# Two blocks on one core: the first sublayer's start in a new order, and all low parts of weights on VectorE

## The chip, the cores and the metric

The kernel runs on one core of a Trainium2 chip. The metric is the device time of one execution, in microseconds. Three runs of the kernel before took 2796.14, 2797.77 and 2798.36 us; their median is 2797.77 us. One execution was profiled as well; its span, from its first to its last instruction, is 2793.1 us.

## The reference

Two transformer blocks on 512 tokens of 1024 features, in float32. Only the beginning matters in detail:

```python
c_act = silu(c)
mod = (c_act @ w_mod[l] + b_mod[l]).reshape(1, 9, 1024)
h = rmsnorm(x, g_norm[l, 0]) * (1 + mod[:, 1]) + mod[:, 0]
x = x + 0.5 * mod[:, 2] * swiglu(h, w_ffn1_gu[l], w_ffn1_down[l])
```

Then, for each of two layers, a mixer (windowed attention, a gated recurrence and short convolutions), and a second feed-forward part; then a second block: a mixer of latent attention (a softmax over 768 keys) and gated linear attention, also over 256 context tokens, and a feed-forward part whose gate goes through a 3 x 3 convolution. Each part begins with an RMS norm, scaled and shifted by vectors that are products of a condition with a matrix.

## The kernel before

Features lie on the partitions, tokens along the free axis: x is eight chunks `X[0..7]` of 128 x 512. A weight comes as units of 128 x 1024 or less, in their order of use, by DMA from SyncE into four buffers (`raw`). Products are made in three passes of rounded parts: each weight and each input is split into a high part (`whi`, a rounded copy, made by ScalarE) and a low part (`wlo`, the value less its high part), and high x high, high x low and low x high are added up in one PSUM bank. There are four `whi` and four `wlo` buffers, so splits run up to three units ahead.

`split_next` (line 454) makes the parts of the next unit. The low part is VectorE's (`split`, line 509) in most of the first block. For the first eight units, for the second block's mixer (key `x`) and for its feed-forward part (key `20`) it is GpSimd's (line 465); the eight have 896 columns, most of the others 1024.

The unit list also holds the rows of `w_mod`: a modulation vector's 128 values are a dot product on VectorE of a 128 x 1024 tile with the condition's row (line 515), and a read of the accumulator, both in `dot`. `mod_unit` adds the bias (line 527) and, for the scale, makes (1 + m) g (line 529).

`start` (line 1986) is the head. Products of ones run first; the squares of the eight chunks are made by ScalarE and added up by VectorE in two sums (lines 572 to 577); eight one-column products add them over the features (line 1994); root and reciprocal follow, `diag` puts the 512 values on a diagonal (line 612), and `spread` brings them to all partitions by a product (line 620). Then, chunk by chunk: two dots, the modulation of the chunk (`modulate_chunk`, lines 645 to 648: x A bc on VectorE, high part on ScalarE, low part on VectorE), and 21 products into seven banks (lines 2009 to 2011).

At the end of a sublayer the last four of eight out-chunks are made in token halves, so that the next norm's first half runs beside the second half's products. Line 679 adds a product to the residual, lines 576 and 577 square and add up, line 584 sums over the features.

A scheduler that lists instructions by estimated times sets the order on each engine; an engine then runs its instructions in that order, and one that waits holds up those behind it. So the order of the text is not always that of the engine. Units are loaded as buffers come free, in their order, on SyncE's queue.

## Time and profile before

| | |
|---|---|
| runs | 2796.14 to 2798.36 us, median 2797.77 |
| profiled execution | span 2793.1 us; its own total is not recorded, the runs are 3.0 to 5.3 us above the span |
| TensorE, products | 2737.6 us (98%), 13858 instructions |
| VectorE | 1617.8 us (58%) |
| ScalarE | 1025.3 us (37%) |
| GpSimd | 322.4 us (12%), 137 low parts of 2.35 us mean |
| read from HBM | 345.21 MB, 127 GB/s over the span |

A busy share is an average over 2.8 ms of stages with different limits, so the table alone names only the engine that is busy nearly all the time. What can change is read from the stretches in which it is not, and from the instruction that ends its wait there. A product in float32 can be two instructions in the trace. Busy times of neighbours overlap a little: two instructions of 0.75 us can start 0.67 us apart.

### The profile page before, as it was taken

What the parts mean: (1) busy time and instruction counts of PE and PEld (TensorE: products, weight loads), DVE (VectorE), ACT (ScalarE), POOL (GpSimd) and SP (SyncE); (2) the same over time, 40 slices, a digit from 0 to 9 for tenths busy, and PEclk for the clock granted to TensorE, in tenths of its full rate; (3) what the DMA queues carried; (4) which work ended last, traced back from release to release, by engine and by line L of the source; (5) the groups of instructions that cost most, each with busy time, mean ns of one, the idle gap of its engine ahead of it and who ended that gap; (6) DMA issues with size and microseconds to landing.
All of it is one profiled execution on the core that took longest, in us unless ns stands there. A gap on an engine that the chain in (4) does not pass through costs nothing.

```text
span 2793.1 us, 34824 instructions
## 1 busy us (share of the span) xinstructions
PE 2737.6 (98%) x13858; PEld 2259.1 (81%) x13858; DVE 1617.8 (58%) x2723; ACT 1025.3 (37%) x1606; POOL 322.4 (12%) x141
## 2 busy tenths in 40 slices
PE   8999999999999999999999999999999999999998
PEld 6888897888888988889788888888777777888887
DVE  8554468664444744446857755463466675673445
ACT  3322236442222422223644222343343664432322
POOL 2000000000000000000000000013322113344442
PEclk9999999999999999999999999999999999999999
DMA  6644444344444444444424665423221213232332
GB/s 253 202 142 143 147 142 133 109 147 147 136 146 148 140 149 139 142 150 146 136 69 142 204 203 176 127 80 113 84 83 63 85 34 116 81 95 94 93 94 63
DMA packets 105890, 355.85 MB, mean 127 GB/s; under 512 B 11776, under 2 KB 14976, under 8 KB 105472
## 3 DMA queue, kind: packets, MB, share of 16 engines
q1 hardware_dynamic: 105728, 353.64, 39.3%
q8 instruction: 108, 1.77, 0.3%
q14 instruction: 54, 0.44, 0.0%
HBM read 345.21 MB, written 8.39 MB: 127 GB/s over the span
## 4 chain that ended last, share of the span: by engine, by line
PE 90%; DVE 7%; ACT 2%; issue 1%; DMA 0%; DVEq 0%; ACTq 0%
PE pb L503 27%; PE pb L505 27%; PE pb L504 27%; PE pb L1776 1%; ACT farena L400 1%; PE pd L1748 1%; DVE r L648 1%; PE pd L1765 1%; DVE farena L515 1%; DVE mod L527 1%; PE pb L620 1%; DVE r L511 1%; PE pb L1433 1%; PE pb L1434 1%; PE pb L1435 1%
## 5 line engine op out<-in xcount | busy, mean ns | idle before, releaser
L503 PE MATMUL pb<-r,wlo 128*128 128x512 f32 (+1 forms) x3360 | 1251.1, 373 | 0.4 <-ACT r L647 0.4
L504 PE MATMUL pb<-r,whi 128*128 128x512 f32 (+1 forms) x3360 | 1241.7, 370 | 2.1 <-DVE r L648 2.1
L505 PE MATMUL pb<-r,whi 128*128 128x512 f32 (+1 forms) x3360 | 1242.4, 370 | 0.0
L503 PEld LDWEIGHTS pb<-r,wlo 128*128 128x128 f32 x3360 | 632.1, 188 | 128.0 <-issue 8.0
L504 PEld LDWEIGHTS pb<-r,whi 128*128 128x128 f32 x3360 | 632.4, 188 | 121.3 <-DVE r L648 2.9
L505 PEld LDWEIGHTS pb<-r,whi 128*128 128x128 f32 x3360 | 632.3, 188 | 119.9 <-issue 0.2
L465 POOL TENSOR_TENSOR wlo<-raw,whi 128x1024 fp32r<-128x1024 f32 (+2 forms) x137 | 322.2, 2353 | 2442.4 <-ACT whi L464 2426.0
L510 ACT ACTIVATE whi<-raw 128x1024 fp32r<-128x1024 f32 (+1 forms) x313 | 324.1, 1036 | 663.2 <-issue 403.7
L511 DVE TENSOR_TENSOR wlo<-raw,whi 128x1024 fp32r<-128x1024 f32 (+1 forms) x313 | 373.8, 1195 | 163.1 <-ACT whi L510 162.3
L515 DVE CUSTOM_DVE_ANT_0 raw<-raw,farena 128x1024 f32<-128x1024 f32 x176 | 215.1, 1223 | 192.0 <-DMA raw<-wmod 142.3
L679 DVE SCALAR_TENSOR_TENSOR farena<-pb,mod,farena 128x512 f32<-128x512 f32 (+1 forms) x176 | 114.6, 652 | 235.7 <-PE pb L505 235.7
L464 ACT ACTIVATE whi<-raw 128x1024 fp32r<-128x1024 f32 (+2 forms) x137 | 140.2, 1024 | 206.9 <-issue 113.1
L503 PE MATMUL pb<-xr,wlo 128*128 128x512 f32 (+1 forms) x520 | 188.0, 362 | 0.0
L505 PE MATMUL pb<-xr,whi 128*128 128x512 f32 (+1 forms) x520 | 186.7, 359 | 0.0
L504 PE MATMUL pb<-xr,whi 128*128 128x512 f32 (+1 forms) x520 | 186.6, 359 | 0.0
L770 DVE TENSOR_TENSOR farena<-pb,farena 128x512 f32<-128x512 f32 x110 | 75.8, 690 | 180.1 <-PE pb L505 161.1
L400 ACT ACTIVATE farena<-pb 128x512 f32<-128x512 f32 x93 | 55.6, 598 | 336.9 <-PE pb L505 335.5
L822 DVE SCALAR_TENSOR_TENSOR farena<-pb,vecs,farena 128x441 f32<-128x441 f32 (+2 forms) x176 | 122.3, 695 | 74.7 <-ACT farena L814 69.3
L504 PEld LDWEIGHTS pb<-xr,whi 128*128 128x128 f32 x520 | 97.9, 188 | 16.4
L503 PEld LDWEIGHTS pb<-xr,wlo 128*128 128x128 f32 x520 | 97.6, 188 | 16.6
L505 PEld LDWEIGHTS pb<-xr,whi 128*128 128x128 f32 x520 | 97.8, 188 | 16.1
L511 DVE TENSOR_TENSOR r<-farena,r 128x512 fp32r<-128x512 f32 (+1 forms) x87 | 83.1, 959 | 20.5 <-ACT r L510 20.1
(273 smaller groups left out, 2026.7 us busy)
## 6 DMA issues: line engine op xcount, KB each, us to landing
raw<-gu SPq DMA_DIRECT2D x213, 512.0 KB, 3.5
raw<-wmod SPq DMA_DIRECT2D x128, 512.0 KB, 3.5
raw<-dn SPq DMA_DIRECT2D x80, 448.0 KB, 3.4
raw<-wada SPq DMA_DIRECT2D x48, 512.0 KB, 3.8
raw<-dn SPq DMA_DIRECT2D x40, 512.0 KB, 3.7
raw<-w2a SPq DMA_DIRECT2D x34, 512.0 KB, 3.5
raw<-win SPq DMA_DIRECT2D x32, 512.0 KB, 3.5
raw<-wout SPq DMA_DIRECT2D x24, 512.0 KB, 3.4
```

The source lines that it names most:

```text
L400: i = self.A.activation(out, in_, func, **k).ins
L464: self.A.activation(h[:, :n], raw[:, :n], AF.Copy)
L465: self.nc.gpsimd.tensor_tensor(lo[:, :n], raw[:, :n], h[:, :n].bitcast(F32), op=SUB)
L503: self.T.matmul(acc, lhsT=lo[:, s], rhs=xh[:, tok], start=i == 0, stop=False)
L504: self.T.matmul(acc, lhsT=h[:, s], rhs=xl[:, tok], start=False, stop=False)
L505: self.T.matmul(acc, lhsT=h[:, s], rhs=xh[:, tok], start=False, stop=i == n - 1)
L510: self.A.activation(hi, src, AF.Copy)
L511: self.V.tensor_tensor(lo, src, hi.bitcast(F32), op=SUB)
L515: self.V.tensor_tensor_reduce(out=out, in0=raw, in1=row, scale=1.0, scalar=0.0, op0=MUL, op1=ADD, accum_out=col)
L679: self.V.scalar_tensor_tensor(x, acc[:, :n], gate[:, d:d + 1], x, op0=MUL, op1=ADD)
L770: self.V.tensor_tensor(a[:, :], acc[:, :], g[:, :], op=MUL)
L822: self.V.scalar_tensor_tensor(o, g[:, r0 + i - 1:r1 + i - 1, c0 + j - 1:c1 + j - 1], self.v(f"cw{i}{j}", f), o, op0=MUL, op1=ADD)
```

## The change

Three things are changed. First, `split_next` has one branch: every low part of a weight is VectorE's. Second, `start` is written in another order: VectorE squares three of the eight chunks, four pairwise sums go into 16 one-column products, the table of roots is loaded by ScalarE between squares, the first dot stands ahead of the diagonal, and of each chunk's 21 products the seven of high with high parts come first. Units are split one chunk ahead rather than two. Third, bias and scale of a modulation value are one instruction each; 1 + bias is made once (`b1`). Comments and docstrings are taken out as well, so lines move up by three to four and, from `start` on, down.

```diff
@@ split_next
-            if self.nsplit < KD or key[0] in ("20", "x"):
-                self.A.activation(h[:, :n], raw[:, :n], AF.Copy)
-                self.nc.gpsimd.tensor_tensor(lo[:, :n], raw[:, :n], h[:, :n].bitcast(F32), op=SUB)
-            else:
-                self.split(raw[:, :n], h[:, :n], lo[:, :n])
+            self.split(raw[:, :n], h[:, :n], lo[:, :n])
@@ mod_unit
             if l == 0 and j < 16:
-                V.tensor_tensor(m, m, self.v("b_mod0", j), op=ADD)
-                if j >= 8:
-                    V.scalar_tensor_tensor(m, m, 1.0, self.v("g00", j - 8), op0=ADD, op1=MUL)
+                if j < 8:
+                    V.tensor_scalar(m, m, self.v("b_mod0", j), None, op0=ADD)
+                else:
+                    V.tensor_scalar(m, m, self.b1[:, j - 8:j - 7], self.v("g00", j - 8), op0=ADD, op1=MUL)
@@ program
+    p.b1 = p.cp.tile([P, 8], F32, name="b1")
+    p.V.tensor_scalar(p.b1[:, :], p.v("b_mod0")[:, 8:16], 1.0, None, op0=ADD)
...
-    p.table("sqrt")
@@ start
-    sq = [p.f(), p.f()]
+    ss = p.banks.get()
+    sums = []
+
+    def add(a, b):
+        p.V.tensor_tensor(a[:, :], a[:, :], b[:, :], op=ADD)
+        b.done()
+        sums.append(a)
+
+    sq = [p.f() for _ in range(KD)]
+    own = (3, 5, 7)
     for k in range(KD):
-        p.sq_add(sq[k % 2][:, :], p.X[k], k < 2)
-    ss = p.banks.get()
+        if k not in own:
+            p.A.activation(sq[k][:, :], p.X[k], AF.Square)
+    for k in own:
+        p.V.tensor_tensor(sq[k][:, :], p.X[k], p.X[k], op=MUL)
+    p.table("sqrt")
+    for a, b in ((3, 0), (5, 1), (7, 2), (4, 6)):
+        add(sq[a], sq[b])
     for j in range(4):
-        for i in range(2):
-            p.T.matmul(ss[:, j:j + 1], lhsT=sq[i][:, j * P:(j + 1) * P], rhs=p.ones[:, 0:1], start=i == 0, stop=i == 1)
+        for i, a in enumerate(sums):
+            p.T.matmul(ss[:, j:j + 1], lhsT=a[:, j * P:(j + 1) * P], rhs=p.ones[:, 0:1], start=i == 0, stop=i == 3)
+    for a in sums:
+        a.done()
+    p.split_next()
     r = p.rstd(ss[:, :4], 4, D)
     ss.done()
-    for b in sq:
-        b.done()
-    bc = p.spread(p.diag(r, 4), 4)
+    dg = p.diag(r, 4)
+    p.split_next()
+    bc = p.spread(dg, 4)
     accs = [p.banks.get() for _ in range(FIRST)]
     for k in range(KD):
+        if k == 0:
+            p.modulate_chunk(p.X[k], FULL, bc, A, sh, h[k], k)
         wh, wl = p.take("00", "k", k)
-        p.modulate_chunk(p.X[k], FULL, bc, A, sh, h[k], k)
+        if k:
+            p.modulate_chunk(p.X[k], FULL, bc, A, sh, h[k], k)
...
         for i in range(FIRST):
             s = slice(i * P, (i + 1) * P)
-            p.T.matmul(accs[i][:, :], lhsT=wl[:, s], rhs=hi[:, :], start=k == 0, stop=False)
-            p.T.matmul(accs[i][:, :], lhsT=wh[:, s], rhs=lo[:, :], start=False, stop=False)
-            p.T.matmul(accs[i][:, :], lhsT=wh[:, s], rhs=hi[:, :], start=False, stop=k == KD - 1)
+            p.T.matmul(accs[i][:, :], lhsT=wh[:, s], rhs=hi[:, :], start=k == 0, stop=False)
+        for i in range(FIRST):
+            s = slice(i * P, (i + 1) * P)
+            p.T.matmul(accs[i][:, :], lhsT=wl[:, s], rhs=hi[:, :], start=False, stop=False)
+            p.T.matmul(accs[i][:, :], lhsT=wh[:, s], rhs=lo[:, :], start=False, stop=k == KD - 1)
         p.rt += 1
-        p.advance(min(k + 2, KD))
+        p.advance(k + 1)
```

How this moves instructions on VectorE shows at three places. The first is between the root's reciprocal and the first chunk's modulation, in the kernel before (`farena` holds float32 tiles, `mod` the modulation values, `pb_75` the spread values):

```order
L594 RECIPROCAL small<-small 128x4
L612 TENSOR_TENSOR farena<-cst,small 128x512
L515 ISA farena,mod_130<-farena 128x1024
L515 ISA mod_130 128x1
L527 TENSOR_TENSOR mod_130<-mod_130,vecs 128x1
L515 ISA farena,mod_130<-farena 128x1024
L515 ISA mod_130 128x1
L527 TENSOR_TENSOR mod_130<-mod_130,vecs 128x1
L529 SCALAR_TENSOR_TENSOR mod_130<-mod_130,vecs 128x1
L645 SCALAR_TENSOR_TENSOR farena<-farena,mod_130,pb_75 128x512
```

And in the changed kernel:

```order
L591 RECIPROCAL small<-small 128x4
L511 ISA farena,mod_130<-farena 128x1024
L511 ISA mod_130 128x1
L524 TENSOR_SCALAR mod_130<-mod_130,vecs 128x1
L609 TENSOR_TENSOR farena<-cst,small 128x512
L511 ISA farena,mod_130<-farena 128x1024
L511 ISA mod_130 128x1
L526 TENSOR_SCALAR mod_130<-mod_130,b_151,vecs 128x1
L642 SCALAR_TENSOR_TENSOR farena<-farena,mod_130,pb_75 128x512
L507 TENSOR_TENSOR wlo<-raw,whi 128x896
```

The diagonal (L612, now L609) stood right behind the reciprocal; now a dot, its read and its bias stand in front of it. The first weight's low part is now in this row, behind the modulation.

The second place is VectorE's row of one chunk, from the second modulation to the third, before (`r_88` and up are input parts):

```order
L645 SCALAR_TENSOR_TENSOR farena<-farena,mod_130,pb_75 128x512
L515 ISA farena,mod_130<-farena 128x1024
L515 ISA mod_130 128x1
L648 SCALAR_TENSOR_TENSOR r_91<-farena,mod_130,r_90 128x512
L527 TENSOR_TENSOR mod_130<-mod_130,vecs 128x1
L515 ISA farena,mod_130<-farena 128x1024
L515 ISA mod_130 128x1
L527 TENSOR_TENSOR mod_130<-mod_130,vecs 128x1
L529 SCALAR_TENSOR_TENSOR mod_130<-mod_130,vecs 128x1
L645 SCALAR_TENSOR_TENSOR farena<-farena,mod_130,pb_75 128x512
```

And in the changed kernel, from the second modulation to the third:

```order
L642 SCALAR_TENSOR_TENSOR farena<-farena,mod_130,pb_75 128x512
L511 ISA farena,mod_130<-farena 128x1024
L511 ISA mod_130 128x1
L645 SCALAR_TENSOR_TENSOR r_91<-farena,mod_130,r_90 128x512
L524 TENSOR_SCALAR mod_130<-mod_130,vecs 128x1
L511 ISA farena,mod_130<-farena 128x1024
L511 ISA mod_130 128x1
L507 TENSOR_TENSOR wlo<-raw,whi 128x896
L526 TENSOR_SCALAR mod_130<-mod_130,b_151,vecs 128x1
L511 ISA farena,mod_130<-farena 128x1024
L511 ISA mod_130 128x1
L642 SCALAR_TENSOR_TENSOR farena<-farena,mod_130,pb_75 128x512
```

A weight's low part (L507) is in the row, three small instructions have become two, and three dots stand between these two modulations; two between each pair on average.

The third place is VectorE's row at the end of the first block, from the first half's modulation to the last sums of squares of the second half, before:

```order
L645 SCALAR_TENSOR_TENSOR farena<-farena,small,pb_75 128x256
L577 TENSOR_TENSOR farena<-farena 128x256
L648 SCALAR_TENSOR_TENSOR r_101<-farena,mod_132,r_100 128x256
L648 SCALAR_TENSOR_TENSOR r_111<-farena,mod_132,r_110 128x256
L645 SCALAR_TENSOR_TENSOR farena<-farena,small,pb_75 128x256 x4
L648 SCALAR_TENSOR_TENSOR r_113<-farena,mod_132,r_112 128x256
L648 SCALAR_TENSOR_TENSOR r_115<-farena,mod_132,r_114 128x256
L648 SCALAR_TENSOR_TENSOR r_117<-farena,mod_132,r_116 128x256
L648 SCALAR_TENSOR_TENSOR r_119<-farena,mod_132,r_118 128x256
L679 SCALAR_TENSOR_TENSOR farena<-pb_79,mod_131,farena 128x256
L679 SCALAR_TENSOR_TENSOR farena<-pb_73,mod_131,farena 128x256
L577 TENSOR_TENSOR farena<-farena 128x256 x4
```

And in the changed kernel:

```order
L645 SCALAR_TENSOR_TENSOR r_113<-farena,mod_132,r_112 128x256
L645 SCALAR_TENSOR_TENSOR r_115<-farena,mod_132,r_114 128x256
L642 SCALAR_TENSOR_TENSOR farena<-farena,small,pb_75 128x256 x2
L574 TENSOR_TENSOR farena<-farena 128x256
L645 SCALAR_TENSOR_TENSOR r_117<-farena,mod_132,r_116 128x256
L645 SCALAR_TENSOR_TENSOR r_119<-farena,mod_132,r_118 128x256
L574 TENSOR_TENSOR farena<-farena 128x256
L507 TENSOR_TENSOR wlo<-raw,whi 128x1024
L676 SCALAR_TENSOR_TENSOR farena<-pb_73,mod_131,farena 128x256
L507 TENSOR_TENSOR wlo<-raw,whi 128x1024
L574 TENSOR_TENSOR farena<-farena 128x256 x2
L574 TENSOR_TENSOR xf<-xf,farena 128x256
```

Two low parts of weights now stand around the last residual (L676), ahead of the last adds of squares (L574); before, GpSimd had them.

## Rows read from the trace of the kernel before

**Rows 1.** Busy time by stretches: engines' busy us (instructions), clock, DMA share, GB/s.

```profile
22.46:70.76 48.30, 44.50 (x168) 32.98 (x169) 46.58 (x72) 12.96 (x17) 14.78 (x7) 0.94 0.59 209
70.76:1844.00 1773.24, 1768.86 (x8686) 1461.72 (x8685) 1024.14 (x1755) 615.94 (x974) 2.40 (x1) 1.00 0.45 145
1844.00:1868.00 24.00, 17.22 (x119) 16.76 (x119) 19.53 (x40) 10.70 (x24) 7.55 (x3) 0.86 0.36 121
...
1960.00:2200.00 240.00, 226.97 (x1254) 183.85 (x1253) 140.89 (x270) 106.18 (x185) 65.38 (x28) 1.00 0.26 85
2200.00:2320.00 120.00, 113.54 (x866) 93.03 (x865) 77.45 (x147) 80.26 (x133) 11.30 (x5) 0.97 0.17 55
...
2395.00:2418.00 23.00, 19.76 (x129) 18.64 (x129) 16.46 (x28) 9.99 (x19) 9.68 (x4) 0.85 0.27 92
...
2440.00:2480.00 40.00, 40.00 (x173) 32.15 (x172) 30.96 (x43) 15.45 (x20) 16.89 (x7) 1.00 0.29 94
```

**Rows 2.** Timeline of the squares: start us, us, engine, line, idle before and releaser.

```profile
8.48 3.21 ACT L576 ACTIVATE farena<-farena 128x512 f32<-128x512 f32 x6
...
9.13 3.70 DVE L577 TENSOR_TENSOR farena<-farena 128x512 f32<-128x512 f32 x6 [8.12 <-ACT farena L576]
```

**Rows 3.** Timeline from the feature sums to the first product.

```profile
12.88 1.90 PE L1994 MATMUL pb<-ones,farena 128*128 128x1 f32 x14 [0.22 <-DVE farena L577]
...
16.14 2.07 PE L620 MATMUL pb<-farena,ones 128*128 128x512 f32 x2 [1.35 <-DVE farena L612]
...
20.81 0.75 DVE L645 SCALAR_TENSOR_TENSOR farena<-farena,mod,pb 128x512 f32<-128x512 f32 x1
...
22.46 1.62 PE L2009 MATMUL pb<-r,wlo 128*128 128x512 f32 x3 [4.25 <-ACT r L647]
```

**Rows 4.** VectorE's groups, 20.81 to 63.66 us: xcount | busy us, mean ns | idle before.

```profile
L515 DVE CUSTOM_DVE_ANT_0 farena<-farena 128x1024 f32<-128x1024 f32 x14 | 17.0, 1215 | 0.0
...
L645 DVE SCALAR_TENSOR_TENSOR farena<-farena,mod,pb 128x512 f32<-128x512 f32 x8 | 6.0, 747 | 0.4
```

**Rows 5.** Timeline of one chunk's small adds and GpSimd's low part beside them.

```profile
23.23 2.10 POOL L465 TENSOR_TENSOR wlo<-raw,whi 128x896 fp32r<-128x896 f32 x1 [2.75 <-DMA raw<-gk]
23.29 2.06 DVE L527 TENSOR_TENSOR mod<-mod,vecs 128x1 f32<-128x1 f32 x1
...
26.52 0.16 DVE L527 TENSOR_TENSOR mod<-mod,vecs 128x1 f32<-128x1 f32 x1
```

**Rows 6.** VectorE's groups by form, 100 to 1840 us, in the first block.

```profile
L511 DVE TENSOR_TENSOR wlo<-raw,whi 128x1024 fp32r<-128x1024 f32 x242 | 295.6, 1222 | 130.2 <-ACT whi L510 129.7
...
L511 DVE TENSOR_TENSOR wlo<-raw,whi 128x896 fp32r<-128x896 f32 x64 | 69.7, 1089 | 31.1 <-ACT whi L510 30.9
...
L648 DVE SCALAR_TENSOR_TENSOR r<-farena,mod,r 128x256 fp32r<-128x256 f32 x80 | 34.7, 479 | 0.6 <-ACT r L647 0.6
```

**Rows 7.** Timeline of the first border.

```profile
1845.98 2.56 DVE L577 TENSOR_TENSOR farena<-farena 128x256 f32<-128x256 f32 x1
...
1851.26 5.05 DVE L648 SCALAR_TENSOR_TENSOR r<-farena,mod,r 128x256 fp32r<-128x256 f32 x2
...
1861.55 0.59 PE L584 MATMUL pb<-ones,farena 128*128 128x1 f32 x2 [5.64 <-DVE farena L577]
```

**Rows 8.** Timeline of the second border.

```profile
2395.59 2.37 DVE L612 TENSOR_TENSOR farena<-cst,small 128x256 f32<-128x256 f32 x1
...
2403.86 4.88 DVE L648 SCALAR_TENSOR_TENSOR r<-farena,mod,r 128x256 fp32r<-128x256 f32 x4
```

**Rows 9.** Timeline in the linear attention and in the softmax stretch.

```profile
2031.88 2.29 DVE L1571 COPY small<-farena 128x8 f32<-128x8 f32 x1
...
2035.56 1.16 PE L1599 MATMUL pb<-farena 128*128 128x128 f32 x8 [2.14 <-DVE farena L1572]
...
2212.93 2.44 DVE L511 TENSOR_TENSOR r<-farena,r 128x512 fp32r<-128x512 f32 x1
...
2216.57 1.54 PE L1765 MATMUL pd<-cst,farena 128*128 128x128 f32 x6 [2.77 <-ACT farena L400]
```

## The prediction

> **What bounds the kernel now.** I read the busy time by stretches first. TensorE is busy nearly everywhere, so only the places count where it stands or runs at a lower clock. From 70.8 to 1844 us it stands 4.4 of 1773 us at clock 1.00 [rows 1]; there VectorE already makes all low parts of weights, and nothing of the change acts there. What is left is the head (up to 70.8 us), two borders between sublayers (1844 to 1868 and 2395 to 2418), the linear-attention stretch (1960 to 2200, 13.0 us idle), and the softmax stretch (2200 to 2320, 6.5 us idle).
>
> In the timeline of the head the first product stands at 22.46 us [rows 3]; the stretch that ends at 70.76, where the second set of weights begins, has 168 products. At full clock 173 products take 40 us [rows 1], 0.231 us each, so 168 need 38.8 us; they took 48.3. VectorE is busy 46.6 of these 48.3 us: its chain per feature chunk sets the pace. The first modulation starts at 20.81 us [rows 3], the eighth at 63.66, where the stretch of rows 4 ends: 42.85 us, that is 7 periods of 6.12 us.
>
> What fills a period: two dot products, one modulation, one low part of the modulated input, and small adds [rows 4]. One small add of 128x1 in each period takes 2.06 us, and it is over as soon as GpSimd's low part (23.23 + 2.10 = 25.33 us) is over; the same add without GpSimd beside it takes 0.16 us [rows 5]. So 1.9 us of the 6.12 are a wait for GpSimd.
>
> The same pattern stands in the second block, where GpSimd makes all low parts. An add of 256 columns takes 2.56 us at 1845.98, and two low parts of the norm take 5.05 us together [rows 7], against 0.48 each in the first block [rows 6]; TensorE then waits 5.64 us for the sums at 1861.55 [rows 7].
>
> **The change, part by part.** Durations are from the profiled execution, whose span is 2793.1 us; the median of the runs is 2797.77, 4.7 us more, and I leave these 4.7 as they are.
>
> *Squares and sums.* Before, ScalarE squares X[2] to X[7] from 8.48 us on at 0.535 us a piece, and the adds end at 12.83 [rows 2]. Now VectorE squares three of eight. The third add waits for ScalarE's square of X[6], which had landed by 10.6 us; then a square and an add of VectorE (0.6 each) follow. From the order and these bounds the last add ends between 12.7 and 13.2; I take 12.9. So the squares gain nothing: the arrival of X holds them. But 16 instead of 8 products sum over the features, and 14 of them stand behind the last add instead of 7. Seven products (14 instructions) took 1.90 us [rows 3], so 14 take 3.8 and end at 16.7 instead of 14.78. From the end of the sums to the spread product were 1.36 us (16.14 - 14.78). Now one dot product with its read and add (1.22 + 0.25) stands ahead of the diagonal: 16.7 + 1.36 + 1.5 = 19.55. The spread takes 2.07 [rows 3], the first modulation comes at 21.65 instead of 20.81, and the first product 1.65 behind it (as 22.46 - 20.81), at 23.3. This step loses 0.8 us.
>
> *The chunk stage.* A period of VectorE is now two dots at 1.22, a modulation at 0.75 and a low part of the input of the same form, at 0.67 net of its overlap [rows 4], two small ops at 0.17 and a weight's low part of 896 columns at 1.0 to 1.09 [rows 6]: 5.2 us. Seven periods are 36.4; the last modulation comes at 58.05, its products can start at 59.7. TensorE by itself: 23.3 + 38.8, and the low clock at the start cost 48.3 x (1 - 0.94) = 2.9 [rows 1]: 65.0. The two are now nearly equal, and since periods with three and with one dot alternate in the new order, I add 1 us of waits: the stage ends at 66.0 instead of 70.76. Products with the high parts come first now, so a low part has 7 x 0.231 = 1.6 us more time; that is why I let its 1.0 us not stand in front of the first product. **Head: -4.8 us**, from -6.5 (no waits, sums quicker) to -2.5 (the sums run at half clock, the first product at 24.5).
>
> VectorE is 97% busy in this stage, and the low parts go onto it. The Trainium skill (Perfetto Trace Analysis, section Optimizing Scalar/DVE Operations) says that work of a saturated VectorE may be worth moving to ScalarE or even GpSimd, the reverse of this change; the same passage warns that these two share a port. By the first sentence a period would be 6.12 + 1.0 and the stage 7 us longer; the rows on the 2.06 us add decide for the second here.
>
> *First border.* VectorE's row from 1845.98 on leads to the sums at 1861.55. The waits that go: 2.56 - 0.48 and 5.05 - 0.96, together 6.2. Three low parts of weights now stand in its row before the last sums, 3 x 1.22 = 3.7 (one of them ahead of the diagonal). The sums come 2 to 2.5 us earlier. In these 24 us the granted clock is 0.86, worth 24 x 0.14 = 3.4 us of full clock; it falls behind the 5.64 us wait. If the shorter wait leaves the clock up, that comes back too. Idle times of 2.1 us stand at clock 1.00, one of 2.77 does not [rows 1, 9]; the new one is about 2.4 to 3.5. I take **-3**, from -2 to -5.5.
>
> *Second border.* Waits that go: 2.37 - 0.48 and 4.88 - 1.9 [rows 8], 4.9; three low parts come in, 3.6. So 1.3, and the clock there (0.85 over 23 us) is worth 3.4 more. TensorE's idle time is 3.2 in all. The borders of the first block have the same code with low parts on VectorE, and no lower clock. I take **-3**, from -1.3 to -5.
>
> *Linear attention.* 28 low parts stand in these 240 us, VectorE is busy 141 us of them [rows 1]; with 28 x 1.22 = 34 more it is at 73% at most. Of the 13.0 us that TensorE waits some are plainly GpSimd's: a copy of 128x8 takes 2.29 us at 2031.88, and TensorE waits 2.14 us behind it [rows 9]. On the other side each low part is 1.2 us in VectorE's row, plus a wait for its high part (129.7 us for 242 of them, 0.54 each, in the first block [rows 6]), and in the new order it often stands right ahead of that same copy. I take **-2.5**: from -9 to +12.
>
> *Softmax.* A low part of a value waits until 2215.3 (2.44 us), a scale behind it, and TensorE 2.77 us [rows 9]. In its place a weight's low part of 768 columns (0.9 us) stands behind the row maximum. I take **-1**, from -6 (with the clock, 120 x 0.03) to +3.
>
> *Second feed-forward part.* From 2418 on TensorE never waits. In its fullest stretch VectorE is busy 31 of 40 us with 7 low parts on GpSimd [rows 1]; 7 x 1.22 more is 39.5 less its waits. Cover is thin there, but eight banks and four weight buffers lie between; I cost it at 0, and at +8 if the cover is gone. The eight bias sums that are folded into single instructions are in the 0.17 above.
>
> Sum: -4.8 - 3 - 3 - 2.5 - 1 = -14.3, 2797.8 - 14.3 = **2783.5 us**.
>
> **Rivals.** *Everything that GpSimd holds up comes back, clock included*: -6.5 - 5.5 - 5 - 7 - 5 = -29, 2769 us. For it: TensorE's waits there follow directly on stretched instructions. Against it: 129 low parts must go somewhere.
>
> *Only the head gains*: in the second block the low parts take on VectorE what the waits took before. 2797.8 - 4.8 = 2793. For it: at both borders the two sums differ by 1.3 to 2.5 us only.
>
> *VectorE becomes the limit in the linear attention (slower)*: its low parts queue ahead of instructions that TensorE waits for, at 1.22 + 0.54 = 1.76 each. If 15 of 28 do, 26 us come in and some 7 of GpSimd's go: +19, less 2.5 in the head and 3.3 at the borders, +13 or 2811 us. It decides from about 8 of 28 (14 against 12.8). Against it: the mixers of the first block have chains of the same sort with low parts on VectorE, and the whole block has 4.4 us of waits.
>
> *VectorE's saturation in the head (slower)*: the 2 us add is its own cost, and 1.0 us a period is added: 7 x 1.0 + 0.8, 2805 us. This is the first sentence of the passage named above. Against it stands the 0.16 us of the same add in the same period.
>
> **How the numbers follow.** Forecast 55% (its own range 2776 to 2791), everything back 13%, only the head 20%, linear attention 8%, saturated head 2%, a full VectorE in the feed-forward part 2%. 0.2% is 5.6 us, about what can be told from no change: faster is below 2792.2. The forecast and "everything" are faster, of "only the head" a bit under half: 77%. Same 13%, slower 10%. The range 2768 to 2797 takes in the two gaining cases and the head alone.
>
> **What would show it.** Right: no 128x1 instruction of VectorE over 0.3 us in the head, a period near 5.2 us, the first product near 23.3 and the end of the stage near 66; the wait before the sums at the first border under 4 us, and the clock at the second border at 1.00. Wrong: a first product after 24.5; TensorE waiting for weights' low parts in the feed-forward part; waits of more than 13 us between the projections and the softmax, with a weight's low part just ahead of what is waited for.

## The result

The changed kernel took 2719.28 to 2720.95 us in four runs, median 2719.66; the kernel before had a median of 2796.95 in four runs. The ratio is 0.9732 [0.972, 0.9743]. It is faster, by 77 us and not by the 14 us that I forecast; the time lies far below the lower end of my range.

The profile page of the changed kernel, the span and the engines, then the granted clock in 40 slices:

```profile
span 2717.6 us, 34690 instructions
PE 2686.7 (99%) x13874; PEld 2262.7 (83%) x13874; DVE 1671.1 (61%) x2854; ACT 1022.1 (38%) x1603; POOL 0.2 (0%) x4
...
PEclk9999999999999999999999999999999999999999
```

TensorE's busy time fell by 51 us with 16 products more. Fewer waits alone don't make busy time smaller; a higher clock or a shorter step from product to product does. The clock gives some 10 us (below); for the rest the products themselves must follow each other faster. Three stretches of 200 us, in the first block and in the second block's feed-forward part, before (columns as in [rows 1]):

```profile
100.00:300.00 200.00, 200.00 (x859) 160.79 (x858) 100.59 (x174) 53.65 (x67) 0.00 (x0) 1.00 0.47 147
...
1500.00:1700.00 200.00, 200.00 (x861) 160.78 (x860) 133.71 (x200) 57.73 (x76) 0.00 (x0) 1.00 0.61 195
...
2450.00:2650.00 200.00, 200.00 (x859) 160.76 (x858) 103.57 (x144) 64.02 (x77) 85.52 (x36) 1.00 0.30 93
```

and after:

```profile
100.00:300.00 200.00, 200.00 (x879) 164.66 (x878) 99.48 (x171) 53.27 (x65) 0.00 (x0) 1.00 0.46 150
...
1500.00:1700.00 200.00, 200.00 (x882) 164.85 (x881) 133.55 (x203) 57.87 (x76) 0.00 (x0) 1.00 0.62 206
...
2450.00:2650.00 200.00, 200.00 (x878) 164.63 (x877) 126.50 (x162) 59.12 (x70) 0.00 (x0) 1.00 0.30 96
```

TensorE is busy all the time at clock 1.00 in each of them, and does 19 to 21 products more. In the first two GpSimd does nothing in either kernel, and no line of the program that runs there has changed. The changed kernel's timeline shows which products are short (start us, us, engine, line, tiles):

```profile
122.67 0.39 PE L501 MATMUL pb<-r,whi 128*128 128x512 f32 x1
122.90 0.39 PE L499 MATMUL pb<-r,wlo 128*128 128x512 f32 x1
123.12 0.39 PE L500 MATMUL pb<-r,whi 128*128 128x512 f32 x1
123.35 0.39 PE L501 MATMUL pb<-r,whi 128*128 128x512 f32 x1
123.58 0.40 PE L499 MATMUL pb<-xr,wlo 128*128 128x512 f32 x1
...
123.81 0.39 PE L500 MATMUL pb<-xr,whi 128*128 128x512 f32 x1
124.04 0.40 PE L501 MATMUL pb<-xr,whi 128*128 128x512 f32 x1
124.27 0.39 PE L499 MATMUL pb<-xr,wlo 128*128 128x512 f32 x1
124.50 0.40 PE L500 MATMUL pb<-xr,whi 128*128 128x512 f32 x1
124.74 0.39 PE L501 MATMUL pb<-xr,whi 128*128 128x512 f32 x1
```

Read the starts, not the durations: products with inputs from the slots `r` follow each other at 0.2275 us (122.67 to 123.58, four steps), those with inputs from `xr` at 0.232 (123.58 to 124.74, five steps). Before, 859 products in 200 us are 0.233 each. One thing in which they differ is where the tiles lie. The diff adds a tile, `b1`, of eight columns, 32 bytes per partition. Everything allocated behind it moves by 32 bytes. Start of the tiles in bytes per partition, from the built programs:

```
             slot r0          whi (first)       wlo (first)       xr
before        77952            173408            189792           206560
after         77952            173440            189824           206592
r0 - whi, remainder by 256:   before  32, after   0
xr - whi, remainder by 256:   before 128, after 128
```

(Slots follow at 2048 bytes, weights' tiles at 4096, blocks of a weight at 512.) The other places answer to the rows of before as follows. For the head: the first product and the end of the stage, the short adds of one chunk, and the row of the stage and of all behind it up to the first border (columns as in [rows 1]):

```profile
22.42 3.35 PE L2027 MATMUL pb<-r,whi 128*128 128x512 f32 x7 [1.59 <-ACT r L644]
...
63.74 0.39 PE L499 MATMUL pb<-r,wlo 128*128 128x512 f32 x1
```

```profile
25.48 0.21 DVE L524 TENSOR_SCALAR mod<-mod,vecs 128x1 f32<-128x1 f32 x1
25.61 0.27 DVE L526 TENSOR_SCALAR mod<-mod,b,vecs 128x1 f32<-128x1 f32 x1
25.79 1.08 DVE L507 TENSOR_TENSOR wlo<-raw,whi 128x896 fp32r<-128x896 f32 x1
...
30.52 1.09 DVE L507 TENSOR_TENSOR wlo<-raw,whi 128x896 fp32r<-128x896 f32 x1
```

```profile
22.42:63.74 41.32, 41.18 (x169) 32.90 (x169) 41.14 (x75) 13.78 (x19) 0.00 (x0) 0.95 0.71 255
...
63.74:1809.33 1745.59, 1741.08 (x8686) 1468.56 (x8685) 1023.85 (x1756) 614.98 (x974) 0.00 (x0) 1.00 0.45 147
```

The stage ends at 63.74 instead of 70.76 [rows 1], and two of its low parts stand 4.73 us apart (25.79, 30.52; from the first at 25.79 to the last at 55.31 they are six periods of 4.92). The add that took 2.06 us [rows 5] takes 0.21, the one behind it 0.27. First border, linear attention, softmax, second border and the full feed-forward stretch after, each from and to the product that has the number of the one with which the stretch of [rows 1] begins and ends (16 added for the head; near the borders some products have changed places; columns as there):

```profile
1809.33:1825.02 15.69, 14.61 (x120) 14.15 (x118) 13.73 (x32) 10.54 (x23) 0.00 (x0) 1.00 0.43 141
1916.31:2145.72 229.41, 224.50 (x1254) 184.41 (x1252) 151.05 (x298) 106.19 (x184) 0.00 (x0) 1.00 0.27 89
2145.72:2259.73 114.01, 109.33 (x867) 90.53 (x865) 76.69 (x153) 80.11 (x133) 0.00 (x0) 1.00 0.18 58
2333.31:2348.62 15.31, 15.31 (x129) 15.26 (x128) 14.11 (x29) 8.01 (x17) 0.00 (x0) 1.00 0.30 100
2371.45:2410.22 38.77, 38.77 (x173) 32.11 (x172) 35.21 (x50) 15.92 (x21) 0.00 (x0) 1.00 0.37 121
```

The first four were 24, 240, 120 and 23 us long: they are shorter by 8.3, 10.6, 6.0 and 7.7. TensorE stands 1.1, 4.9, 4.7 and 0 us in them, against 6.8, 13.0, 6.5 and 3.2, and the clock is 1.00 in all, where it was 0.86, 1.00, 0.97 and 0.85.

### The profile page after: what moved, and what is told of

It reads as the page before. It is cut to its first block, busy times and chain, and to the rows that moved or that the text cites. A ratio compares the mean times of both kernels' runs of the same rounds, so it can differ in the third digit from the quotient of the medians.

```text
span 2717.6 us, 34690 instructions
## 1 busy us (share of the span) xinstructions
PE 2686.7 (99%) x13874; PEld 2262.7 (83%) x13874; DVE 1671.1 (61%) x2854; ACT 1022.1 (38%) x1603; POOL 0.2 (0%) x4
## 3 DMA queue, kind: packets, MB, share of 16 engines
q8 instruction: 108, 1.77, 0.3%
## 4 chain that ended last, share of the span: by engine, by line
PE 93%; DVE 4%; ACT 2%; issue 1%; DMA 0%; SPq 0%; DVEq 0%; ACTq 0%
PE pb L499 28%; PE pb L501 28%; PE pb L500 28%; PE pb L1773 1%; PE pd L1745 1%; PE pd L1762 1%; ACT farena L400 1%; PE pb L617 1%; PE pb L1167 1%; PE pb L1640 0%; DVE wlo L507 0%; PE pb L1114 0%; PE pb L1151 0%; PE pb L581 0%; PE pb L1430 0%
## 5 line engine op out<-in xcount | busy, mean ns | idle before, releaser
L499 PE MATMUL pb<-r,wlo 128*128 128x512 f32 (+1 forms) x3360 | 1236.6, 369 | 1.2 <-DVE wlo L507 1.1
L500 PE MATMUL pb<-r,whi 128*128 128x512 f32 (+1 forms) x3360 | 1229.2, 367 | 0.0
L501 PE MATMUL pb<-r,whi 128*128 128x512 f32 (+1 forms) x3360 | 1228.8, 366 | 0.0
L506 ACT ACTIVATE whi<-raw 128x1024 fp32r<-128x1024 f32 (+2 forms) x450 | 464.2, 1032 | 828.1 <-issue 448.5
L499 PEld LDWEIGHTS pb<-r,wlo 128*128 128x128 f32 x3360 | 632.8, 189 | 114.4 <-issue 7.6
L507 DVE TENSOR_TENSOR wlo<-raw,whi 128x1024 fp32r<-128x1024 f32 (+2 forms) x450 | 535.7, 1191 | 211.8 <-ACT whi L506 210.4
L676 DVE SCALAR_TENSOR_TENSOR farena<-pb,mod,farena 128x512 f32<-128x512 f32 (+1 forms) x176 | 114.9, 653 | 210.5 <-PE pb L501 210.2
L573 ACT ACTIVATE farena<-farena 128x256 f32<-128x256 f32 (+1 forms) x97 | 44.8, 467 | 84.3 <-DVE farena L676 84.3
L644 ACT ACTIVATE r<-farena,mod 128x256 fp32r<-128x256 f32 (+1 forms) x119 | 55.3, 514 | 51.2 <-DVE farena L642 50.7
L400 ACT ACTIVATE farena<-farena 128x512 f32<-128x512 f32 (+2 forms) x89 | 50.5, 604 | 58.6 <-DVE farena L819 47.7
```

Source lines behind the costliest of these rows:

```text
L400: i = self.A.activation(out, in_, func, **k).ins
L499: self.T.matmul(acc, lhsT=lo[:, s], rhs=xh[:, tok], start=i == 0, stop=False)
L500: self.T.matmul(acc, lhsT=h[:, s], rhs=xl[:, tok], start=False, stop=False)
L501: self.T.matmul(acc, lhsT=h[:, s], rhs=xh[:, tok], start=False, stop=i == n - 1)
L506: self.A.activation(hi, src, AF.Copy)
L507: self.V.tensor_tensor(lo, src, hi.bitcast(F32), op=SUB)
```

## The experiments

Three theories came from this. **A**: the place of the weights' parts in SBUF sets the pitch of the products. **B**: GpSimd, idle in the changed kernel, had slowed TensorE. **C**: the new order of instructions does it. Medians of `before` beside these runs were 2793.1 to 2795.2 us.

**Only the 32 bytes**, in the kernel before (`b_pad32`):

```diff
     nc.sync.dma_start(p.vecs[:, :], d["vecs"])
+    pad = p.cp.tile([P, 8], F32, name="pad")
+    p.V.memset(pad[:, :], 0.0)
```

> The kernel before with one more tile of 32 bytes per partition, nothing else. It moves everything that is allocated behind it by 32 bytes, as the changed kernel's tile of first modulations does: the parts of the weights then start at a multiple of 64 bytes instead of 32 past one. Theory A (the place of the weights in SBUF sets the pitch of the products): the pitch falls from 0.233 to about 0.227 us, and with some 11,600 products (3 x 3360 + 3 x 520, and others) of 5.5 ns the time falls by 55 to 70 us, to 2730 to 2742; most of the whole gain. Theory B (GpSimd, which still makes 137 low parts here, slows TensorE over the whole program): no change, 2797. Theory C (the new order of instructions does it): no change, 2797.

2757.8 us, ratio 0.9872 [0.9857, 0.9887]: 35 us gone by a tile that nothing reads. Its stretch from 100 to 300 us has 880 products, here above that of the next run:

```profile
100.00:300.00 200.00, 200.00 (x880) 164.73 (x879) 103.06 (x178) 54.61 (x67) 0.00 (x0) 1.00 0.46 150
...
100.00:300.00 200.00, 200.00 (x860) 161.24 (x859) 98.35 (x170) 52.31 (x64) 0.00 (x0) 1.00 0.44 144
```

TensorE, VectorE and ScalarE run their instructions in the same order with the tile as without it, in this pair of kernels and in the next, but for one memset more on VectorE; so C falls for this part. So A is right at least in part, but 35 us is short of what I expected and of the 77. I had counted all products; only those of 512 columns became shorter. By form, the three groups of products of 512 columns with slots (2606 each) have means of 399, 395 and 395 ns before and 394, 391 and 390 in the changed kernel, those of 256 columns 286, 284 and 284 against 285, 284 and 285.

**The changed kernel with 32 bytes more** (`a_pad32`): the same two lines in the changed kernel. r0 - whi has remainder 224 by 256 then, where it is 32 in the kernel before.

> The changed kernel with 32 bytes more in front of the weights' parts, so that they start 32 bytes past a multiple of 64 again, as before. Theory A: the pitch goes back to 0.233 us, and the time to 2775 to 2790, where the sum of the prediction had it (2783.5). Theories B and C: no change, 2720.

2760.97 us, ratio 0.9886 [0.9869, 0.9902], with 860 products in 100 to 300 us. So the place is worth 41 us there, which agrees with the count: 3 x 2606 products of 512 columns with slots, at 0.233 - 0.2275 us, are 43. What is left, 32 us, is more than twice my sum of 14.3, and the time lies below the 2775 to 2790 that I expected of A. (35 and 41 us for the same 32 bytes: which part of the difference is more than noise is open.)

**Only the low parts on VectorE**, no address moved (`b_lowV`):

```diff
-            if self.nsplit < KD or key[0] in ("20", "x"):
-                ...
-            else:
-                self.split(raw[:, :n], h[:, :n], lo[:, :n])
+            self.split(raw[:, :n], h[:, :n], lo[:, :n])
```

> The kernel before with all low parts of weights on VectorE and nothing else of the change; no address moves. Theory A: the pitch stays 0.233 us; the gain is that of the waits alone, by the prediction 1.9 us a chunk in the head less about 1.0 for the low part (-4 to -6) and -9.5 in the second block, so 2781 to 2786. Theory B: GpSimd has nothing left to do, so the pitch falls to 0.227 and the time to 2722 to 2735. Theory C: like A, without a fall of the pitch.

2759.25 us, ratio 0.9877 [0.9862, 0.9892]. The pitch stays (859 products in 100 to 300 us), so B, as an effect on the products, is refuted; yet the gain is 34 us and not 11 to 16. The scheduler orders some instructions anew in this run (at 351 of TensorE's 13858 places stands another one), so the low parts' engine is not quite all that changes. From 1500 to 2600 us before, and the same 5594 products in this run (columns as in [rows 1]):

```profile
1500.00:2600.00 1100.00, 1070.48 (x5594) 881.09 (x5593) 647.75 (x1047) 431.98 (x667) 233.16 (x98) 0.99 0.35 111
```

```profile
1492.53:2563.32 1070.79, 1060.92 (x5594) 873.31 (x5592) 680.83 (x1144) 431.62 (x667) 0.00 (x0) 1.00 0.35 114
```

TensorE's idle time falls from 29.5 to 9.9 us, and the first border, 24 us before, is 15.6 in this run (1836.48 to 1852.12 by the number of products), although VectorE is busy for 33 us more. The clock, read in stretches of 20 us, was 0.83, 0.90, 0.93 and 0.83 before in those that begin at 1860, 2200, 2220 and 2400 us, which loses 3.4 + 2.0 + 1.4 + 3.4 = 10.2 us; in this run it is 1.00 in all between 460 and 2740. The first stage ends at 63.61, 7.1 us earlier. 7.1 + 19.6 + 10.2 = 36.9, and the spans of the two profiled executions differ by 37.1 (2793.1 and 2756.0); the medians differ by 33.8.

**Low parts on VectorE, and GpSimd kept busy beside it** (`b_lowV_gp`): GpSimd makes the same difference once more, into a tile that nothing reads.

```diff
             self.split(raw[:, :n], h[:, :n], lo[:, :n])
+            if self.nsplit < KD or key[0] in ("20", "x"):
+                self.nc.gpsimd.tensor_tensor(self.spare[:, :n], raw[:, :n], h[:, :n].bitcast(F32), op=SUB)
```

> The kernel before with all low parts of weights on VectorE, and GpSimd still makes the same 137 differences, now into a spare tile that nothing reads. With low parts on VectorE and an idle GpSimd the time was 2759.3, 34 us below before. Theory D (what cost the 34 us is that GpSimd's instructions hold up VectorE's while they run): the stretched instructions come back beside the added low parts, and the time is that of before or more, 2790 to 2815. Theory E (the gain is that GpSimd's low parts were late, 2.1 us and more each behind a slow queue, and the products waited for them): 2757 to 2765.

2850.37 us, ratio 1.0197 [1.0182, 1.0212]: 91 us more than with an idle GpSimd, although nobody waits for what GpSimd makes, and TensorE, VectorE and ScalarE run their instructions in the same order as in `b_lowV`. So theory D, though above the 2790 to 2815 that it gave: what costs is that GpSimd's instructions run beside VectorE's. One other way is open to them: GpSimd reads `raw` and `whi`, which then come free later. ScalarE waits eight times for that, 23.8 us in all; TensorE waits for a weight's low part once from 1500 us on, 2.6 us. What share of the 91 us comes that way no run tells. The timeline shows it (start us, us):

```profile
2028.29 2.39 POOL L466 TENSOR_TENSOR spare<-raw,whi 128x1024 f32<-128x1024 f32 x1 [5.75 <-ACT whi L509]
2028.94 2.82 DVE L510 TENSOR_TENSOR wlo<-raw,whi 128x1024 fp32r<-128x1024 f32 x1
...
2034.21 1.23 DVE L510 TENSOR_TENSOR wlo<-raw,whi 128x1024 fp32r<-128x1024 f32 x1 [2.46 <-ACT whi L509]
2034.31 3.40 POOL L466 TENSOR_TENSOR spare<-raw,whi 128x1024 f32<-128x1024 f32 x1 [3.63 <-ACT whi L509]
```

Where GpSimd is first, it ends at 2030.68 and VectorE's low part at 2031.76, 1.08 later: VectorE had waited for all of it. Where VectorE is first, it takes its 1.23 and GpSimd 3.40, a little over 1 us more than its 2.39. The Trainium skill (SBUF — State Buffer, section Who interferes with whom) says that the two engines hold a shared pair of ports by an exclusive lock; by that rule both pairs come out as they do, and the trace agrees. The price shows in TensorE's waits, two of them from 1500 us on (line waited for, us in total, times, longest):

```profile
PE pb L619 <- DVE farena L611: 11.7, 6, 4.0
PE pb L1642 <- DVE farena L1627: 5.9, 3, 3.4
```

and in the clock, which is between 0.74 and 0.92 in ten stretches of 20 us from 1860 to 2460.

Not every instruction of VectorE is held up. In the kernel before one of GpSimd's low parts stands beside an addition with one input from a PSUM bank (`pb`):

```profile
2433.53 2.42 POOL L465 TENSOR_TENSOR wlo<-raw,whi 128x1024 fp32r<-128x1024 f32 x1 [0.82 <-ACT whi L464]
...
2434.00 0.69 DVE L770 TENSOR_TENSOR farena<-pb,farena 128x512 f32<-128x512 f32 x1
```

It takes 0.69 us, as elsewhere. Counted over that trace, 110 of VectorE's instructions with an input from PSUM began beside a low part of GpSimd and had time to end beside it: none was held up. Of 49 with inputs from SBUF alone 43 ended only behind it; the other six are of one or two columns (three reciprocals, two instructions with a scalar and a read of the accumulator).

**Which place counts.** Eight rows of 48 products at the end of the changed kernel, from one tile that starts at a multiple of 64 bytes (`a_bench`), weights from column w on and inputs from column x on:

```python
CASES = ((0, 2048), (8, 2048), (0, 2056), (8, 2056), (16, 2048), (4, 2048), (0, 2052), (0, 2048))
for w, x in CASES:
    for i in range(48):
        o = w + 128 * (i % 8)
        p.T.matmul(bk[:, :], lhsT=p.xt[:, o:o + 128], rhs=p.xt[:, x:x + 512], ...)
```

> The changed kernel with eight rows of 48 products at its end (128x128 weights in eight blocks by turns, 128x512 inputs, one bank a row, everything from one tile that starts at a multiple of 64 bytes). Start of weights and of inputs, in bytes past a multiple of 64 (or 128): row 1 0 and 0, row 2 weights 32, row 3 inputs 32, row 4 both 32, row 5 weights 64, row 6 weights 16, row 7 inputs 16, row 8 as row 1. Theory A, weights' version: rows 2, 4 and 6 at about 0.233 us a product, the others at 0.227. Theory A, inputs' version: rows 3, 4 and 7 at 0.233. Theories B and C: all rows at the same pitch, 0.227 us. The whole is some 90 to 100 us longer than the changed kernel, 2810 to 2820.

Each row ends with a copy of its bank by ScalarE; the distance of two copies is the time of the later row (start us first):

```profile
2724.86 0.60 ACT L1991 ACTIVATE farena<-pb 128x512 f32<-128x512 f32 x1 [11.63 <-PE pb L1989]
2736.05 0.60 ACT L1991 ACTIVATE farena<-pb 128x512 f32<-128x512 f32 x1 [10.60 <-PE pb L1989]
2747.25 0.60 ACT L1991 ACTIVATE farena<-pb 128x512 f32<-128x512 f32 x1 [10.60 <-PE pb L1989]
2758.17 0.60 ACT L1991 ACTIVATE farena<-pb 128x512 f32<-128x512 f32 x1 [10.32 <-PE pb L1989]
2769.36 0.60 ACT L1991 ACTIVATE farena<-pb 128x512 f32<-128x512 f32 x1 [10.60 <-PE pb L1989]
2780.57 0.60 ACT L1991 ACTIVATE farena<-pb 128x512 f32<-128x512 f32 x1 [10.60 <-PE pb L1989]
2791.68 0.60 ACT L1991 ACTIVATE farena<-pb 128x512 f32<-128x512 f32 x1 [10.52 <-PE pb L1989]
2802.61 0.60 ACT L1991 ACTIVATE farena<-pb 128x512 f32<-128x512 f32 x1 [10.33 <-PE pb L1989]
```

(The whole took 2805.75 us, a little less than I expected.) Rows 4 (both moved by 32) and 8 (none) take 10.92 and 10.93 us, 0.2276 a product; the others 11.11 to 11.21, 0.2315 to 0.2335. Row 5, with weights at 64 bytes, is slow too. So neither version of A as I had put it holds: not the place of the weights or of the inputs, but the distance between the two (A2).

Sixteen and seventeen rows more looked for its unit (`a_bench2`, `a_bench3`), the same loop with other pairs.

> The changed kernel with sixteen rows of 48 products at its end, as in the run with eight rows, where rows with equal remainders took 0.2276 us a product (weights and inputs both 0, both 32) and rows with different ones 0.2315 to 0.2335, also weights at 64 and inputs at 0. Inputs less weights, in bytes: rows 1 to 11 have 0, 8, 32, 64, 96, 120, 128, 256, 384, 512, 1024; row 12 has 128 with both at 32; rows 13 to 15 have -32, -96, -124; row 16 has 0. Theory A2 (the distance of weights and inputs counts, not the place of either): fast where it is a multiple of some power of two. If that is 128, rows 1, 7 to 12 and 16 take 0.2276 us and the others 0.231 to 0.234; if it is 256, rows 7, 9 and 12 are slow as well; if 512, row 8 too. Theory A1 (the place of the weights counts): rows 13 to 15 alone are slow, and the eight rows have spoken against it already.

> As the sixteen rows, with seventeen others; inputs less weights in bytes: 0, 64, 64, 320, 576, -64, -192, 192, 128, -128, 16, 160, 224, 240, -256, 768, 0. Theory A2 with 256 bytes: rows 1, 15, 16 and 17 at 0.2267 to 0.2277 us a product, the others at 0.231 to 0.240. What is open is 64: it took 0.2290 once, and -64 0.2331. If a second remainder is fast, rows 2 to 5 and 7 (all 64 past a multiple of 256) take under 0.230 and row 6 (192) does not; if 0.2290 was one row's chance, rows 2 and 3 differ from it, at 0.233.

| inputs less weights, bytes | us a product |
|---|---|
| 0, -256, 256, 512, 768, 1024 | 0.2267 to 0.2277 |
| 64, 320, 576 | 0.2288 to 0.2294 |
| -192, -64, 192 | 0.2331 to 0.2333 |
| 128 (also with both at 32), -128, 384 | 0.2321 to 0.2333 |
| 8, 16, -16, 32, -32, 96, -96, -124, 160, 224, 240 | 0.2315 to 0.2356 |
| 120 | 0.2400 |

Multiples of 256 are fast, in all six; 128 and 384 are not. 64 past a multiple of 256 is nearly fast where the weights lie at a multiple of 256 from the tile's start, and slow at -192, where they lie 192 past one: distance alone doesn't tell the whole, and that stays open.

**In the whole kernel**: distance 0 with neither weights nor inputs at a multiple of 64 (`b_both96`: 96 bytes more in front of the slots, 32 behind them), the old distance with the weights at a multiple of 128 (`b_front32`: 32 bytes in front of the slots), and distance 128 (`a_pad128`: 128 bytes in front of the weights, in the changed kernel).

> The kernel before with the inputs' slots r0 to r35 moved by 96 bytes and all behind them by 128: inputs and weights' parts then both start 96 bytes past a multiple of 128, none at a multiple of 64. Theory A2 (their distance counts): pitch 0.2276 us, and the time as with 32 bytes in front of the weights' parts alone (2757.8), 2752 to 2764. Theory A1 (the place of the weights counts): nothing changes, 2788 to 2798.

> The kernel before with 32 bytes more in front of the inputs' slots, so that all moves: the weights' parts start at a multiple of 128 as in the changed kernel, the slots 32 past one, their distance is that of before. Theory A1: 2752 to 2764. Theory A2: no gain, pitch 0.233 us, 2788 to 2798.

> The changed kernel with 128 bytes more in front of the weights' parts: every start is still a multiple of 64 and of 128, but slots and weights' parts are now 128 bytes off a multiple of 256 from each other; xr stays 128 off as well. Theory A2 with 256 bytes: the products with the slots are slow again, as with 32 bytes (2761.0), 2752 to 2764. Theory A2 with 128 bytes, and theory A1: 2718 to 2722.

2758.41 us (ratio 0.9867 [0.9852, 0.9881]); 2793.79 (0.9996 [0.9987, 1.0006]); 2758.92 (0.9873 [0.986, 0.9887]). All three as A2 with 256 bytes has it. The first has weights' parts, slots and `xr` off a multiple of 64 and is fast; the other two have their weights at a multiple of 128 and are slow.

**The products that were still slow** (`a_xr128`): `xr` stood at 128 in both kernels. Four small tiles more in front of it bring it to 0.

```diff
-        self.sm = mk("sm", 12)
+        self.sm = mk("sm", 16)
```

> The changed kernel with four more small tiles (128 bytes) in front of xr, the other store of rounded inputs, and nothing else. In the changed kernel the slots r0 to r35 start a multiple of 256 bytes from the weights' parts, xr 128 off one. In the sixteen rows the distances 0, 256, 512 and 1024 took 0.2267 to 0.2277 us, 128 and 384 took 0.2321 to 0.2333, so the 1560 products of weights with xr should be slow still. Theory A2 with 256 bytes: 1560 times about 5.5 ns (less where something else waits) come back, and some of the attention's products with xr: 2709 to 2714 against 2719.7. Theory A2 with 128 bytes, or a distance that counts within one tile only: 2718 to 2721.

2713.86 us (2710.07 to 2715.04), ratio to before 0.9713 [0.97, 0.9726]. The same products as above, in this run:

```profile
123.64 0.39 PE L499 MATMUL pb<-xr,wlo 128*128 128x512 f32 x1
...
123.87 0.39 PE L500 MATMUL pb<-xr,whi 128*128 128x512 f32 x1
124.10 0.39 PE L501 MATMUL pb<-xr,whi 128*128 128x512 f32 x1
124.32 0.39 PE L499 MATMUL pb<-xr,wlo 128*128 128x512 f32 x1
124.55 0.39 PE L500 MATMUL pb<-xr,whi 128*128 128x512 f32 x1
124.78 0.39 PE L501 MATMUL pb<-xr,whi 128*128 128x512 f32 x1
```

Five steps from 123.64 to 124.78 are 0.228 each, as with the slots. 3 x 360 products of 512 columns with `xr`, at 0.232 or 0.233 less 0.2275 us, are 5 to 6 us, the 6 that it gained; I had again counted those of 256 columns. This version beats both kernels.

**Without the new head** (`b_lowV_pad32`): the two edits of `b_lowV` and `b_pad32` together, nothing else.

> The kernel before with all low parts of weights on VectorE and 32 bytes in front of the weights' parts: the changed kernel without its new head (squares by two engines, order of the chunks, short adds). Theory F (the head's gain carries through to the end): in the profiles without the shift the new head reached the 500th product 4.1 us earlier than the low parts alone, so 2722 to 2725 against 2719.7. Theory G (it is given back later, as the profiles of the two without the shift had it, where the 4.1 us had gone by 1630 us): 2717 to 2721.

2719.81 us, ratio 0.9733 [0.972, 0.9747]; the changed kernel has 2719.66. So the new head is worth nothing, as G has it, but not for G's reason. The first product of the feed-forward part, in the changed kernel at 63.74 us, here:

```profile
63.63 0.39 PE L499 MATMUL pb<-r,wlo 128*128 128x512 f32 x1
```

Nothing had been won that could be given back: the 4.1 us that I expected from were read at the 500th product, and the new head issues 16 products more ahead of it.

## Why the prediction was wrong

**The failed step is "At full clock 173 products take 40 us [rows 1], 0.231 us each".** I took the pitch of the products from before as a constant of the chip, and so counted only stalls, low clock and what moves. It is a property of that program's memory map. Some 35 to 41 us of the 77 are this term, which stands nowhere in my sum and in none of my rivals: 2760.97 with the distance off a multiple of 256 and 2719.66 with it on one in the changed kernel, about 2793 and 2757.8 in the one before. What I said of 70.8 to 1844 us, "there VectorE already makes all low parts of weights, and nothing of the change acts there", fails with it: the tile `b1` acts there on every product of 512 columns with a slot, and the same 8686 products take 1745.6 us instead of 1773.2.

**Head, -4.8: the mechanism held, the term was too small.** The stage ends at 63.74, 7.0 us earlier; I had 66.0. The waits of small adds for GpSimd went as predicted. The period is 4.92 us against my 5.2. The first product stands at 22.42 against 23.3. The 1 us of waits that I added "since periods with three and with one dot alternate" came: in every second period (at 33.92, 43.83 and 53.7 us) two steps between products are longer, 1.0 us in all. The 2.3 us by which the stage ends earlier than I had it are 0.9 of the first product, 0.6 of the shorter step (168 times 0.231 less 0.2275) and 0.8 of the clock, 0.95 over 41.3 us where I took 0.94 over 48.3. All 7 us are the low parts': with them alone the first product stands at 20.8 and the stage ends at 63.6. VectorE is busy for 41.14 and TensorE for 41.18 of the 41.32 us of the stage (22.42 to 63.74) in the changed kernel; with both full, a new order had little left to give.

**Borders, -3 and -3; linear attention, -2.5; softmax, -1: the sizes were off.** I had 9.5 us in all; in `b_lowV`, where the pitch is that of before, the four stretches by the number of products are 15.6, 230.9, 114.4 and 15.1 us long, which is 8.4 + 9.1 + 5.6 + 7.9 = 31.0 less; some 1 us of it is lost again between them. By kind it is the 19.6 of waits and the 10.2 of clock above. I set against each stretched instruction the low parts that VectorE takes on, one for one (3.7 us at the first border). For VectorE's own row that came out about right: in the four stretches it takes over 40 low parts, 46.6 us of work, and is busy for 255.6 us instead of 254.3. But TensorE's waits did not follow that sum. Two thirds of the waits went (29.5 to 9.9 us), and all that low parts of weights cost TensorE in the changed kernel from 1500 us on is one wait of 1.1 us, at the first border. That the low parts mostly stand where TensorE needs nothing of VectorE at once, and that the stretched instructions stood where it did, is my reading; no run tests it by itself. And I gave the clock half a sentence ("if the shorter wait leaves the clock up, that comes back too") where every one of the four low stretches went. Nor does the length of one wait tell the clock, as I read it from [rows 1, 9]: at the second border before, TensorE waited 1.9 us at most at a time, and the clock was 0.85.

**Feed-forward, 0: held** as far as waits go; TensorE stands nowhere from 2371.45 to 2410.22 us, with VectorE busy for 35.2 of 38.8.

**The rivals.** "Everything that GpSimd holds up comes back, clock included" was the right one for this part: where it had 29 us, `b_lowV` gained 34. I gave it 13%, because the low parts "must go somewhere". "VectorE becomes the limit" and the saturated head did not happen: the gain of the one-branch edit is of the other sign. The passage that I weighed (the Trainium skill, Perfetto Trace Analysis, section Optimizing Scalar/DVE Operations) names both the remedy and its price. Here the price was the larger: `b_lowV` gains 34 us by the way back, and `b_lowV_gp` loses 91.

## What to carry to other kernels

Before a sum is made from a busy engine's time, ask whether that time per instruction is fixed: compare the count of the same instructions in a full stretch before and after, and look up whether an added tile, however small, moves the operands of the products. For products of float32r with 128 x 128 weights and 512 columns keep the starts of weights and inputs a multiple of 256 bytes apart, for every store that inputs come from. A difference on GpSimd held up nearly every larger instruction of VectorE that reads from SBUF alone until it was over, and none that reads one input from PSUM; where TensorE waited behind that, its clock was lower as well (0.83 to 0.93 in the four stretches above). Taking it away can give far more than a sum of VectorE's row says; look at what TensorE waits for.

## What the runs showed of the hardware

- Products of 128x512 with a weight load each follow at 0.2267 to 0.2277 us where inputs and weights lie a multiple of 256 bytes apart, and at 0.2315 to 0.240 at most other distances; two kernels of 2.8 ms differ by 35 to 41 us by it. Busy times of weight loads don't show it (188 and 189 ns). No run shows why the distance counts. The Trainium skill (SBUF — State Buffer, section Who interferes with whom) lets nothing but the ports shared by VectorE and GpSimd contend; by that rule distance would not count, and the rows speak against it here.
- 137 differences on GpSimd whose results nothing waits for cost 91 us on a VectorE that makes the same ones, 0.67 us each; 128x1024 low parts of VectorE took 1.77 us mean beside them (37 of them, 1900 to 2350 us) and 1.22 without.
- Beside GpSimd's low parts in the kernel before, 43 of 49 instructions of VectorE with inputs from SBUF alone ended only behind them (an add of 128x1 took 2.06 us instead of 0.16), and none of 110 with an input from PSUM (128x512: 0.69 us beside them and elsewhere).
